# A batched 64x64 matmul: seven of sixteen input loads change their DMA queue

## The chip, the core and the metric

The kernel runs on one core of a Trainium2 chip. The metric is the device time of one execution in microseconds (us), lower is better. A core has five engines that work side by side, each through its own list of instructions in order: TensorE (PE in the profile, its weight loads PEld), VectorE (DVE), ScalarE (ACT), GpSimd (POOL) and SyncE (SP). Transfers between the device memory and the core's own memory are issued by one of SyncE, ScalarE and GpSimd, and are then carried out by the core's 16 DMA engines. The profile lists the transfers by the queue of the engine that issued them: q1 for SyncE, q10 for ScalarE, q0 for GpSimd.

## What is computed

```python
def reference(a, b):                       # both (1024, 64, 64), fp32
    return np.matmul(a, b).astype(np.float32)
```

That is 1024 independent products of 64 x 64 matrices. Each input and the output is 16.78 MB.

## The kernel before

The batch is cut into 16 tiles t of 64 matrices (1.05 MB of b and of the output each) and 8 slices s of 128 matrices of a (2.1 MB each), so that slice s serves tiles 2s and 2s+1. The products are taken in bf16 and summed in fp32.

**Loads.** `load_a(s)` (L69 to L78) brings three quarters of a slice by GpSimd's queue, with a cast to bf16 on the way (L73, three transfers that read 0.52 MB and write 0.26 MB each), and the fourth quarter as fp32 by SyncE's (L77). The first slice comes as fp32 by SyncE and ScalarE (L90). `load_b(t)` (L93) brings one tile of b as fp32 in one transfer (L96) into one of three buffers (`B_AHEAD = 3`): even tiles by SyncE's queue, odd ones by ScalarE's. Each of the 128 partitions gets 16 runs of 512 bytes.

**Work of a tile.** `regroup` (L108, L111; L105 for the first slice) puts a slice of a together in bf16 on VectorE; `transpose` (L120 on TensorE, L123 on ScalarE) transposes half of it; `spread(t)` (L133, four copies on VectorE) lays the transposed matrices out as block diagonals in `at_bd`; `cast(t)` turns the tile of b into bf16 (L144, on VectorE but for tile 0; the last tile in four pieces, L149 on VectorE and L151 on ScalarE). `multiply(t)` runs 64 matmuls (L189) in two halves and evacuates each half from PSUM with four copies (L177): on ScalarE, but for two of the eight copies of an odd tile, which VectorE makes; for the last tile four groups of four copies alternate between the two.

**Stores.** A tile's store is one transfer of 1.05 MB in runs of 1 KB (L166), on GpSimd's queue for tiles 0 to 13. Tile 14 goes out in two halves by SyncE, tile 15 in four quarters by ScalarE and SyncE in turn. It is issued one tile late (`HOLD = 2`). Output tiles have eight buffers.

**Order.** The order of the instructions is written out by hand, and each engine takes its own in that order; waits are put in where data or a free buffer is needed. One step t of the main loop reads:

```python
            if t + 1 < n_t:
                spread(t + 1)
                cast(t + 1)
            if t + B_AHEAD < n_t:
                load_b(t + B_AHEAD)
            if half == 0 and 0 < s < n_s - 1 - A_AHEAD:
                load_a(s + 1 + A_AHEAD)
```

then half a transposition, `multiply(t)`, `regroup` and transposition of a later slice, and `store(t - 1)`. Ahead of the loop stand the loads of tiles 0 to 2 of b and slices 0 to 2 of a; the loads of slices 3 and 4 follow the first multiplication. `load_b(t + 3)` fills the buffer of tile t, so it waits for `cast(t)`. On ScalarE an odd load stands, in order, between the evacuations of one tile and the work of the next. On GpSimd there are, besides the start's memsets, only transfers: the loads of a and the stores of tiles 0 to 13.

Of the kernel before, what the change touches and what calls it, by code (L numbers as in the profile page):

```python
# [13 lines left out]
def kernel(  # L14
# [14 lines left out]
    nc = tc.nc  # L29
# [62 lines left out]

    def load_b(t):  # L93
        b_sb = b_pool.tile([128, 16, 128], fp32, name="b_sb")
        queue = nc.scalar if t % 2 else nc.sync
        queue.dma_start(out=b_sb[:], in_=b_v[t])  # L96
        b_tiles[t] = b_sb

# [111 lines left out]
    with tc.manual_schedule():  # L210
        load_first_a()

        nc.vector.memset(warm[:, 0:1], 0.0)
        nc.scalar.copy(warm[:, 1:2], warm[:, 0:1])  # L214
        load_b(0)
        load_b(1)
        nc.vector.memset(bd_tiles[0][:], 0.0)  # L217
        make_identity(nc, identity)
        nc.gpsimd.memset(bd_tiles[1][:, 0], 0.0)
        load_a(1)  # L220
        load_b(2)
        nc.gpsimd.memset(bd_tiles[1][:, 1], 0.0)
        load_a(2)
# [63 lines left out]
```

## Time and profile before

| what | value |
|---|---|
| median of 3 runs | 135.0 us (134.95 to 135.19) |
| span of the profiled execution, first to last instruction | 133.1 us |
| median less span | 1.9 us |
| busy: VectorE, ScalarE, TensorE's matmuls, GpSimd | 94.5, 87.8, 65.7, 33.7 us |
| stores by GpSimd, 14 | median 22.3 us from issue to landing |
| loads of b by SyncE, 8, and by ScalarE, 8 | median 18.4 and 16.8 us from issue to landing |

The span is that of one execution taken by the hardware profiler; the execution's own time is its span and what lies around it, which the profile does not show, so the difference to the median stands for it. The page cuts the span into 40 equal slices; a digit is the busy share in tenths. "From issue to landing" holds the time a transfer stands in its queue as well as the moving. In a timeline, a line gives the start, the duration, the engine, the source line, the operation, what it writes and reads, and in brackets how long the engine stood idle before it and what ended that; a q after the engine's name marks its sequencer, which issues and waits.

### The profile page before, as it was taken

How to read it: one execution, taken by the hardware profiler on the slowest of the kernel's cores; microseconds unless marked ns; L12 is line 12 of the kernel's file. 1: busy time of each engine (PE TensorE's matmuls, PEld its weight loads, DVE VectorE, ACT ScalarE, POOL GpSimd, SP SyncE). 2: the span in 40 equal slices, each digit the busy share in tenths (PEclk: the TensorE clock that was granted, in tenths of full speed). 3: DMA queues.
4: the chain of work that ended last, by engine and by line, in shares of the span. 5: the costliest groups of instructions: out<-in, count | busy, mean ns of one | idle time of the engine just before them, and what ended most of it. 6: DMA issues, size and time to landing. Idle time of an engine off the chain costs nothing.

```text
span 133.1 us, 2837 instructions
## 1 busy us (share of the span) xinstructions
PE 65.7 (49%) x1152; PEld 62.7 (47%) x1152; DVE 94.5 (71%) x120; ACT 87.8 (66%) x161; POOL 33.7 (25%) x43
## 2 busy tenths in 40 slices
PE   0005504990068386059519672986199361776000
PEld 0005304980068275058509562975199360766000
DVE  5930299208999719598999699969999994978100
ACT  3134505899128999919899759696969987099600
POOL 8981000420082072143144022203020410210000
PEclk9999999999559999968996875579756985556855
DMA  3999999999999999999999999999999999999991
GB/s 75 367 332 311 307 312 279 278 307 326 328 307 402 316 322 334 393 385 401 318 282 365 402 397 356 308 307 387 395 396 387 393 396 391 402 403 402 380 339 41
DMA packets 19021, 45.01 MB, mean 338 GB/s; under 512 B 1088, under 2 KB 3136, under 8 KB 19008
## 3 DMA queue, kind: packets, MB, share of 16 engines
q0 software_dynamic: 6832, 20.19, 50.2%
q1 hardware_dynamic: 7120, 14.68, 30.5%
q10 hardware_dynamic: 5056, 9.96, 19.8%
q8 instruction: 9, 0.15, 0.4%
q14 instruction: 4, 0.03, 0.1%
HBM read 33.55 MB, written 16.78 MB: 378 GB/s over the span
## 4 chain that ended last, share of the span: by engine, by line
DMA 54%; DVE 18%; ACT 13%; issue 4%; PE 3%; SPq 1%; DVEq 0%; ACTq 0%
DMA b_sb<-in_b_dram 54%; ACT o_sb L177 9%; DVE at_bd L133 9%; DVE b_bf L144 4%; DVE o_sb L177 3%; PE at_ps L120 2%; ACT at_sb L123 2%; ACT b_bf L144 1%; PE o_ps L189 1%; DVE a_bf L108 1%; SPq L90 1%; DVE a_bf L111 1%; ACT b_bf L151 1%; SPq L96 0%; DVEq L133 0%
## 5 line engine op out<-in xcount | busy, mean ns | idle before, releaser
L177 ACT COPY o_sb<-o_ps 64x512 f32<-64x512 f32 x106 | 61.6, 581 | 9.5 <-PE o_ps L189 8.2
L189 PEld LDWEIGHTS <-at_bd 128*128 128x128 bf16 x1024 | 42.5, 113 | 39.7 <-DVE b_bf L144 26.8
L189 PE MATMUL o_ps<-b_bf,at_bd 128*128 128x64 bf16 x960 | 41.2, 213 | 36.0 <-DVE b_bf L144 25.1
L133 DVE COPY at_bd<-at_sb 32x1024 f32<-32x1024 f32 x64 | 46.6, 728 | 13.6 <-ACT at_sb L123 11.8
L120 PE MATMUL at_ps<-identity,a_bf 128*128 128x128 f32 x128 | 22.5, 350 | 19.3 <-ACT a_bf L105 11.4
L166 POOL DMA_DIRECT2D out_dram<-o_sb x14 | 16.3, 1166 | 55.4 <-ACT at_sb L123 23.0
L120 PEld LDWEIGHTS at_ps<-identity,a_bf 128*128 128x128 f32 x128 | 20.7, 190 | 19.4 <-issue 19.4
L144 DVE CAST b_bf<-b_sb 128x2048 bf16<-128x2048 f32 x14 | 17.5, 1249 | 10.0 <-DMA b_sb<-in_b_dram 9.8
L123 ACT COPY at_sb<-at_ps 128x512 f32<-128x512 f32 x32 | 17.4, 590 | 9.9 <-PE at_ps L120 7.6
L73 POOL DMA_DIRECT2D a_sb<-in_a_dram x21 | 13.3, 650 | 27.3 <-DVE a_bf L108 20.4
L177 DVE COPY o_sb<-o_ps 64x512 f32<-64x512 f32 x14 | 9.7, 690 | 0.3
L108 DVE COPY a_bf<-a_sb 128x3072 bf16<-128x3072 bf16 x7 | 7.4, 1059 | 0.0
L105 ACT CAST a_bf<-o_sb 128x1024 bf16<-128x1024 f32 x2 | 2.1, 1044 | 5.3 <-DMA o_sb<-in_a_dram 5.3
L111 DVE CAST a_bf<-a_raw 128x1024 bf16<-128x1024 f32 x7 | 4.8, 683 | 0.0
L144 ACT CAST b_bf<-b_sb 128x2048 bf16<-128x2048 f32 x1 | 1.9, 1897 | 4.1 <-DMA b_sb<-in_b_dram 4.1
L177 DVE COPY o_sb<-at_ps 64x256 f32<-64x256 f32 x8 | 3.4, 422 | 1.3 <-PE at_ps L189 1.2
L105 DVE CAST a_bf<-o_sb 128x1024 bf16<-128x1024 f32 x2 | 2.6, 1296 | 2.4 <-DMA o_sb<-in_a_dram 2.3
L189 PE MATMUL at_ps<-b_bf,at_bd 128*128 128x64 bf16 x64 | 3.6, 242 | 1.0 <-DVE at_bd L133 1.0
L217 DVE MEMSET at_bd<- 128x4096 f32 x1 | 3.5, 3472 | 0.8 <-issue 0.8
L151 ACT CAST b_bf<-b_sb 128x512 bf16<-128x512 f32 x2 | 1.1, 615 | 4.3 <-DMA b_sb<-in_b_dram 4.3
L177 ACT COPY o_sb<-at_ps 64x256 f32<-64x256 f32 x8 | 2.9, 367 | 0.1
L214 ACT ACT_TABLE_LOAD x1 | 1.3, 1283 | 2.3 <-issue 2.3
(12 smaller groups left out, 6.1 us busy)
## 6 DMA issues: line engine op xcount, KB each, us to landing
out_dram<-o_sb POOLq DMA_DIRECT2D x14, 1024.0 KB, 22.3
a_sb<-in_a_dram POOLq DMA_DIRECT2D x21, 256.0 KB, 16.4
a_raw<-in_a_dram SPq DMA_DIRECT2D x7, 512.0 KB, 19.1
o_sb<-in_a_dram SPq DMA_DIRECT2D x2, 512.0 KB, 6.2
o_sb<-in_a_dram ACTq DMA_DIRECT2D x2, 512.0 KB, 7.3
out_dram<-o_sb SPq DMA_DIRECT2D x2, 512.0 KB, 7.4
out_dram<-o_sb SPq DMA_DIRECT2D x2, 256.0 KB, 7.7
out_dram<-o_sb ACTq DMA_DIRECT2D x2, 256.0 KB, 5.9
```

The costliest lines, as they stand in the source:

```text
L73: nc.gpsimd.dma_start(out=a_sb[:, h, :, :].rearrange("p v k -> p (v k)"), in_=a_v[s, h])
L105: copy(a_bf[:, :, h, :], a_sb[h].rearrange("p (v k) -> p v k", v=16))
L108: nc.vector.tensor_copy(a_bf[:, :, 0:3, :], cast_sb[:].rearrange("p h v k -> p v h k"))
L111: nc.vector.tensor_copy(a_bf[:, :, 3, :], raw[:])
L120: nc.tensor.transpose(at_ps[:, vo, :], a_cols[:, 4 * vo + 2 * j + wl, :], identity[:])
L123: nc.scalar.copy(at_tiles[s][:, j, :, wl, :, :], at_ps[:].rearrange("p vo (g mp) -> p g mp vo", mp=4),)
L133: nc.vector.tensor_copy(bd[rows, :, :, :, h, :].rearrange("p j g wl mo -> p j (g wl) mo"), at_tiles[t // 2][rows, :, half, :, :, :].rearrange(
L144: (nc.vector.tensor_copy if t else nc.scalar.copy)(b_bf[:], b_sb[:])
L166: store_queue(t, lo).dma_start(out=o_v[t, :, lo : lo + n, :], in_=o_sb[:, lo : lo + n].rearrange("p gh j wl n -> p (gh j wl n)"),)
L177: copies[2 * par + wl](dst, src)
L189: nc.tensor.matmul(o_ps[:, gl, g % 2, j, :], at_bd[:, j, g, :, u], b_bf[:, g, 64 * u : 64 * u + 64], start=(u == 0), stop=(u == 1),)
L217: nc.vector.memset(bd_tiles[0][:], 0.0)
```

## The change

Odd tiles of b from tile 3 on are issued by GpSimd instead of ScalarE: seven transfers, 3, 5, 7, 9, 11, 13 and 15. Tile 1 stays on ScalarE's queue and even tiles on SyncE's. Shape, type and buffers are as before; the cast to bf16 stays where it was. In GpSimd's order the load stands where `load_b` stands in the loop: behind the store of tile t - 2 and ahead of the loads of a and the store of tile t - 1.

```diff
     def load_b(t):
         b_sb = b_pool.tile([128, 16, 128], fp32, name="b_sb")
-        queue = nc.scalar if t % 2 else nc.sync
+        queue = nc.sync if t % 2 == 0 else nc.scalar if t == 1 else nc.gpsimd
         queue.dma_start(out=b_sb[:], in_=b_v[t])
         b_tiles[t] = b_sb
```

## The prediction

> **What bounds the kernel now.** I read the page's slices first, then its queues.
>
> ```profile
> DMA  3999999999999999999999999999999999999991
> GB/s 75 367 332 311 307 312 279 278 307 326 328 307 402 316 322 334 393 385 401 318 282 365 402 397 356 308 307 387 395 396 387 393 396 391 402 403 402 380 339 41
> ...
> q0 software_dynamic: 6832, 20.19, 50.2%
> q1 hardware_dynamic: 7120, 14.68, 30.5%
> q10 hardware_dynamic: 5056, 9.96, 19.8%
> ...
> HBM read 33.55 MB, written 16.78 MB: 378 GB/s over the span
> ```
>
> The 16 DMA engines are busy 90% or more in every slice but the first and the last. The rate looks uneven because the loads of a that cast to bf16 are counted by the half they write: q0's 20.19 MB is 14.68 MB of stores plus 21 x 0.262 MB written by casting loads that read twice that. The three queues are GpSimd's (q0), SyncE's (q1) and ScalarE's (q10: 8 tiles of b and 1.57 MB besides). So the kernel is one transfer of 33.55 + 16.78 = 50.33 MB from first to last. Any change that moves the same bytes can only alter three things: the rate, holes in the stream, and its end.
>
> The windows (last two columns: DMA share, GB/s) give the rate without casting loads:
>
> ```profile
> 97.50:100.00 2.50, 2.50 (x42) 2.50 (x40) 2.41 (x4) 2.12 (x4) 0.31 (x1) 0.50 1.02 394
> 105.00:107.50 2.50, 0.00 (x0) 0.00 (x0) 2.44 (x4) 2.44 (x5) 0.04 (x1) 1.00 1.03 392
> 115.00:122.50 7.50, 6.02 (x110) 5.70 (x107) 6.07 (x13) 5.82 (x11) 1.35 (x1) 0.51 1.03 405
> 122.50:127.50 5.00, 0.00 (x0) 0.00 (x0) 1.26 (x3) 2.90 (x8) 0.00 (x0) 0.82 1.04 379
> 127.50:130.00 2.50, 0.00 (x0) 0.00 (x0) 0.00 (x0) 0.00 (x0) 0.00 (x0) 0.50 0.89 312
> ```
>
> Three queues together give 392, GpSimd's stores alone 405. From 127.5 us the stream thins (0.89 and 312): there the last store pieces, issued late, begin to set the time. Who issues them late is in ScalarE's timeline and the chain of waits:
>
> ```profile
> 116.54 1.14 ACT L151 CAST b_bf<-b_sb 128x512 bf16<-128x512 f32 x2 [4.28 <-DMA b_sb<-in_b_dram]
> 117.70 4.74 ACT L177 COPY o_sb<-o_ps 64x512 f32<-64x512 f32 x8
> 122.46 1.89 ACT L177 COPY o_sb<-at_ps 64x256 f32<-64x256 f32 x5
> ...
> 125.52 0.38 ACTq L166 DMA_DIRECT2D out_dram<-o_sb  x1
> ```
>
> ScalarE stands 4.28 us for tile 15 of b (the chain has it issued at 101.78 and landed at 116.46, 14.68 later). Then come 9.06 us of work to the last issue at 125.52. So stream and last chain end nearly together.
>
> **The change part by part.** The odd tiles from 3 to 15 are seven: 7 x 1.049 = 7.34 MB leave q10 for q0.
>
> *ScalarE loses* seven issues: MOVE_SHAPE of 0.02 us, its waits for VectorE's cast (2.0 us over two) and the gaps behind them ("issue", 2.1 us over three). I count 4.1 us of idle ScalarE gone, at nothing: ScalarE then waits longer for tile 15, which is late next.
>
> *GpSimd gains* seven issues. A store of 1024 runs of 1 KB takes it 0.90 us (at 109.24) to 1.85 (at 68.42); a load of a, 0.53. A tile of b is 2048 runs of 512 B, not in the trace: bounds 0.53 and 2 x 1.85 = 3.7 us, and I take 2 x 0.9 = 1.8, the plain store by its number of runs. 7 x 1.8 = 12.6 us stand beside 99 us in which GpSimd is idle. They cost nothing while older transfers wait in q0: its stores land a median 22.3 us after issue, more than six times even 3.7. If q0 ran dry, each would cost 1.8.
>
> The row shows GpSimd's store issue at 0.90 to 0.93 us alone and 1.35 to 1.37 beside VectorE's spreads. The Trainium skill's "SBUF — State Buffer", section "SBUF: two separate sides", speaks against the change here: a DMA issued from GpSimd stops being described while VectorE runs an fp32 SBUF copy, and one issued from ScalarE doesn't. By that rule each load could wait for one spread copy, 0.68 us by the page's fastest spreads, 7 x 0.68 = 4.8 us in all if bare. By the row it is 0.45 a store, under queued stores and so unseen.
>
> *VectorE* pays when GpSimd issues beside it: the regroup copy at L108 reads 0.95 alone and 1.32 in the two places where a store is issued beside it, so 0.37 a load, 2.6 us over seven. That is no path of its own (below).
>
> *GpSimd's order at the start.* The load of tile 3 stands before the loads of a's fourth slice and waits for the cast of tile 0, which ends at 21.6. These three issues now go at 8.3 to 11.6 and would go at about 24. Their slice is needed at 41.7 (L108). Behind the six earlier loads GpSimd's queue holds until 24, and q1 has work, so no hole. Tile 3 itself may come sooner than its 38.8. Cost: nothing; without that cover, 1 MB late is 2.7 us.
>
> *Queue depth.* GpSimd twice stands for an earlier transfer of its own to land (2.1 and 4.8 us, with eight in flight). It will do so more often, behind eight queued transfers: nothing.
>
> *SyncE* issues the same transfers in the same order. With q10 empty in the middle, q1 should hold a larger share, so even tiles, for which VectorE waits now (most of its 9.8 us in six waits, the longest 3.3), come sooner. In a full stream that is only an exchange of places: nothing.
>
> *The new order inside q0* is what costs. An odd tile now lands after every store issued before it. Landing times of single transfers, by their windows (last number: us from issue):
>
> ```profile
> b_sb<-in_b_dram ACTq DMA_DIRECT2D x1, 0.5 KB, 15.7
> out_dram<-o_sb POOLq DMA_DIRECT2D x1, 1024.0 KB, 28.0
> out_dram<-o_sb POOLq DMA_DIRECT2D x1, 1024.0 KB, 29.8
> out_dram<-o_sb POOLq DMA_DIRECT2D x1, 1024.0 KB, 21.2
> ```
>
> (each from a window of its own). The load is tile 11, issued at 77.29, so landed at 93.0. The stores are those of tiles 5, 6 and 10, issued at 68.42, 71.08 and 96.87: they land at 96.4, 100.9 and 118.1. In q0 tile 11 stands behind stores 5 and 6. At 93.0 some 1.9 MB of the two are not yet moved (store 6 whole, store 5 with 3.4 us to go beside other queues): 1.9/0.392 = 4.8 us, so near 97.8, while its cast starts now at 94.63. That is +3.2 for VectorE there. Of it 1.92 is taken back where VectorE waits for tile 14 (at 112.54), which then is no longer late. The rest, 1.3, reaches VectorE's last copies; these end at 123.8 against ScalarE's 125.5, so 1.7 are free: hidden. With the slower copies (tiles 13 and 15, 0.74) it is still about 2.0 against 1.7, so +0.3 at most.
>
> Tile 15 stands behind store 10, so it lands about when that store does, 118.1 instead of 116.46: +1.6 on ScalarE's last chain, and the last issue goes to 127.1. What that does to the end lies between two rows. The last pieces now take 5.7 us (ScalarE's) to 7.5 us (SyncE's) to land in a full stream; with the same wait, +1.6. But a quiet landing is shorter: the first load, 0.52 MB beside another 0.52, lands in 4.5 us, of which 1.05/0.392 = 2.7 is the moving, so 1.8 fixed; 0.26 MB alone would be an estimated 1.8 + 0.7 = 2.5, so 129.6, before today's last landing near 131.8: +0. The nearest row is the window from 127.5: 0.89 busy, so nearer to full than to quiet, and about a third of a delay shows. I take +0.5.
>
> *Rate.* From 392 to 405 for 7.34 MB gains 18.72 - 18.12 = 0.6; from 392 to 379, the slowest full window, loses 0.64. Two queues (97.5, 394) read like three (392), so I take 0.
>
> Sum: 133.1 + 0.5 + 0 = 133.6 for the span. The median is 135.0, so 1.9 lie outside the span, unchanged: **135.5**.
>
> **Rivals.**
>
> 1. *No change (135.0).* Stores to be moved are plenty behind tile 15 (11 to 15, 5.24 MB = 13.4 us), the late issue is wholly covered. For it: landing of 5.7 to 7.5 where 2.5 would do. Against: the thinning after 127.5.
>
> 2. *Faster (134.3).* The mechanism is packets: GpSimd's stores run at 405 alone, the mixture at 392. If a tile of b runs in q0 like a store, 0.6 are gained for 7.34 MB; if all that is moved between 25 and 115 us (90 x 0.392 = 35.3 MB) goes at the two-queue 394, another 90.0 - 89.6 = 0.4. Together 1.0 at most; taken at 0.7. It decides where windows from 60 to 115 us without casting loads read 397 or more and tile 15 lands no later than 117. Against: two queues read 394 only.
>
> 3. *Clearly slower (137).* Odd tiles fall so far behind in q0 that VectorE, which waits for nothing else late in the kernel, becomes the bound: +4.8 at tile 11 instead of +3.2, and 2.6 for slower copies, less 1.9 and 1.7 taken back: +3.8 at the most, 138.8; about half of it, +2, is this rival's time. It decides when VectorE's idle time before L144, 9.8 us now, doubles, and slices before the last two fall under 9.
>
> 4. *It doesn't do what it says*: ScalarE is relieved, but ScalarE waits for data at the end, so relief alone gives 0. That is contained in the first two.
>
> The skill's "DMA: Bandwidth & Descriptors", section "Issuing engines are not separate DMA queues", has all queues run on the same 16 engines, so that another issuer saves issue time alone: by it the sum would be 135.0. The trace shows that the place in a queue matters as well, since store 10, issued 4.9 us before tile 15, lands 1.6 us after it.
>
> **How the numbers follow.** Forecast (slightly slower, 135.3 to 136.3) 0.37; no change 0.20; faster (133.8 to 134.7) 0.28; clearly slower (136.3 to 138.8) 0.15. About 0.2%, 0.27 us, is what a measurement can tell from no change. So faster 0.28, same 0.20, slower 0.52. The range reaches from 134.2 (most of rival 2's 1.0) to 137.2 (135.0 with the tail's full 1.6 and the rate's 0.64), which leaves out some 0.08 on each side. The forecast's own range is 135.3 to 136.3.
>
> **What would show it.** Right: q0 near 27.5 MB, q10 near 2.6; DMA digits still 9; tile 11 landing at 96 to 100, tile 15 near 118; ScalarE's wait before L151 longer or its cast after 118; last issue near 127. Wrong: tile 15 landing at or before 116.5, a hole in the DMA row, GpSimd's issue of a tile of b over 3.7 us, or a rate over 400 in the middle.

## The result, and the profile after

The changed kernel takes 141.34 us (141.25 to 141.52) against 134.97 of the kernel before, +6.4 us; the ratio over all runs is 1.0488, 95% interval 1.0461 to 1.0515. The prediction was 135.5, range 134.2 to 137.2. Times here and below are medians, and differences in us are differences of medians; the ratios are taken over the runs and can lie some 0.2% beside them.

The profile's span grew from 133.1 to 139.2, by 6.1, so the loss is inside it. The slices and queues of the page after:

```profile
DMA  3999999999999999999999999999999999999991
GB/s 87 380 323 308 306 312 301 347 342 297 271 253 312 391 300 286 280 395 389 317 304 272 404 370 289 232 380 384 321 365 395 337 379 400 359 381 397 364 361 37
...
q0 software_dynamic: 8736, 27.53, 64.7%
q1 hardware_dynamic: 7120, 14.68, 30.5%
q10 hardware_dynamic: 1360, 2.62, 5.0%
...
HBM read 33.55 MB, written 16.78 MB: 362 GB/s over the span
```

The bytes are those announced (27.53 and 2.62 MB), and the DMA digits are the same as before, all 9: no hole. Yet the rate over the span fell from 378 to 362. The engines are as busy as before and move less. Late slices, where no casting load is left to blur the count, read 321, 337 or 359 beside others of 395 to 400. The windows there (last two columns: DMA share, GB/s) show where:

```profile
97.50:102.50 5.00, 1.09 (x32) 1.00 (x32) 2.92 (x4) 4.77 (x9) 1.36 (x1) 0.94 1.03 323
102.50:107.50 5.00, 2.15 (x41) 2.15 (x42) 3.40 (x5) 0.22 (x1) 0.89 (x1) 0.50 1.03 397
107.50:112.50 5.00, 4.39 (x80) 4.06 (x78) 4.76 (x7) 4.90 (x10) 1.12 (x1) 0.88 1.03 343
112.50:117.50 5.00, 1.75 (x47) 1.63 (x47) 4.84 (x7) 4.91 (x9) 1.43 (x2) 0.81 1.03 393
120.00:122.50 2.50, 1.52 (x30) 1.36 (x28) 1.47 (x2) 2.17 (x4) 0.00 (x0) 0.50 1.02 336
122.50:127.50 5.00, 3.24 (x59) 2.96 (x57) 4.83 (x8) 3.26 (x6) 1.36 (x1) 0.50 1.01 394
```

Windows near 395 and windows near 335 alternate. The landings of two of the moved loads (last number: us from issue) say what the latter are:

```profile
b_sb<-in_b_dram POOLq DMA_DIRECT2D x1, 1024.0 KB, 22.8
b_sb<-in_b_dram POOLq DMA_DIRECT2D x1, 1024.0 KB, 12.7
```

They are tile 11, issued at 81.15 and landed at 104.0, and tile 15, issued at 111.38 and landed at 124.1; tile 13 between them, issued at 96.27, landed at 113.5. The windows with the low rate are those just before a moved tile lands: GpSimd's queue is then at that tile. Against 397 the first of them loses 5 x (1 - 323/397) = 0.93 us, the third window 0.68, the fifth 0.38: 2.0 us in the middles of three such stretches, out of seven. ScalarE's timeline at the end is that of before, moved by 7.6 us (116.54 to 124.18, and 125.52 to 133.15):

```profile
124.18 1.14 ACT L151 CAST b_bf<-b_sb 128x512 bf16<-128x512 f32 x2 [1.96 <-DMA b_sb<-in_b_dram]
...
133.15 0.38 ACTq L166 DMA_DIRECT2D out_dram<-o_sb  x1
```

### The profile page after: what moved, and what is told of

It reads as the page before. It is cut to its first block, busy times and chain, and to the rows that moved or that the text cites. A ratio compares the mean times of both kernels' runs of the same rounds, so it can differ in the third digit from the quotient of the medians.

```text
span 139.2 us, 2826 instructions
## 1 busy us (share of the span) xinstructions
PE 66.0 (47%) x1152; PEld 63.0 (45%) x1152; DVE 95.2 (68%) x120; ACT 87.3 (63%) x154; POOL 43.1 (31%) x50
## 3 DMA queue, kind: packets, MB, share of 16 engines
q0 software_dynamic: 8736, 27.53, 64.7%
q10 hardware_dynamic: 1360, 2.62, 5.0%
## 4 chain that ended last, share of the span: by engine, by line
DMA 69%; ACT 7%; DVE 6%; issue 5%; POOL 3%; PE 3%; SPq 1%; DVEq 0%; POOLq 0%; ACTq 0%
DMA b_sb<-in_b_dram 46%; DMA a_sb<-in_a_dram 14%; DMA out_dram<-o_sb 8%; ACT o_sb L177 6%; PE o_ps L189 3%; DVE at_bd L133 2%; DVE b_bf L144 2%; POOL a_sb L73 2%; ACT b_bf L144 1%; POOL b_sb L96 1%; DVE o_sb L177 1%; SPq L90 1%; DVE a_bf L108 1%; ACT b_bf L151 0%; DVE a_bf L111 0%
## 5 line engine op out<-in xcount | busy, mean ns | idle before, releaser
L189 PEld LDWEIGHTS <-at_bd 128*128 128x128 bf16 x1024 | 44.8, 116 | 47.8 <-DVE b_bf L144 32.6
L189 PE MATMUL o_ps<-b_bf,at_bd 128*128 128x64 bf16 x960 | 43.4, 218 | 43.8 <-DVE b_bf L144 31.0
L120 PE MATMUL at_ps<-identity,a_bf 128*128 128x128 f32 x128 | 20.7, 330 | 19.5 <-ACT a_bf L105 11.0
L120 PEld LDWEIGHTS at_ps<-identity,a_bf 128*128 128x128 f32 x128 | 18.7, 175 | 19.5 <-issue 19.5
L144 DVE CAST b_bf<-b_sb 128x2048 bf16<-128x2048 f32 x14 | 17.2, 1227 | 13.6 <-DMA b_sb<-in_b_dram 13.3
L166 POOL DMA_DIRECT2D out_dram<-o_sb x14 | 15.5, 1108 | 27.6 <-ACT o_sb L177 14.8
L96 POOL DMA_DIRECT2D b_sb<-in_b_dram x7 | 9.2, 1310 | 37.1 <-DVE b_bf L144 17.7
L73 POOL DMA_DIRECT2D a_sb<-in_a_dram x21 | 14.3, 694 | 17.2 <-DMA b_sb<-in_b_dram 9.6
L111 DVE CAST a_bf<-a_raw 128x1024 bf16<-128x1024 f32 x7 | 5.4, 773 | 0.0
L144 ACT CAST b_bf<-b_sb 128x2048 bf16<-128x2048 f32 x1 | 1.9, 1898 | 4.1 <-DMA b_sb<-in_b_dram 4.1
```

The source lines that it names most:

```text
L73: nc.gpsimd.dma_start(out=a_sb[:, h, :, :].rearrange("p v k -> p (v k)"), in_=a_v[s, h])
L111: nc.vector.tensor_copy(a_bf[:, :, 3, :], raw[:])
L120: nc.tensor.transpose(at_ps[:, vo, :], a_cols[:, 4 * vo + 2 * j + wl, :], identity[:])
L144: (nc.vector.tensor_copy if t else nc.scalar.copy)(b_bf[:], b_sb[:])
L166: store_queue(t, lo).dma_start(out=o_v[t, :, lo : lo + n, :], in_=o_sb[:, lo : lo + n].rearrange("p gh j wl n -> p (gh j wl n)"),)
L189: nc.tensor.matmul(o_ps[:, gl, g % 2, j, :], at_bd[:, j, g, :, u], b_bf[:, g, 64 * u : 64 * u + 64], start=(u == 0), stop=(u == 1),)
```

## The experiments

The first theory was **A**: runs of 512 bytes move more slowly when GpSimd's queue describes them. Its rivals were **B**, that two queues do less than three, and **C**, that the odd tiles' place behind GpSimd's stores is what costs.

**Odd tiles by SyncE** (r1_sp):

```diff
-        queue = nc.sync if t % 2 == 0 else nc.scalar if t == 1 else nc.gpsimd
+        queue = nc.scalar if t == 1 else nc.sync
```

> Odd tiles of b from 3 on go by SyncE's queue, so GpSimd's queue holds what it held before and two queues work in the middle, as in the changed kernel. Theory A (512-byte runs described by GpSimd move more slowly): no loss from GpSimd, the stream stays at 390 to 400 GB/s, time 134 to 136.5 us. Rival B (two queues instead of three, or ScalarE's queue missing): slow like the change, 140 to 142. Rival C (the place of the odd tiles behind GpSimd's stores and loads of a): they stand behind even tiles of b and quarters of a instead, so at most 1 to 2 us over before, 135 to 137.

Measured: 139.39 us, ratio 1.0313 (1.0277 to 1.0348). All three missed. GpSimd carries no tile of b here, and two thirds of the loss (4.4 us) are still there. Its windows show both kinds again, late in the kernel:

```profile
90.00:92.50 2.50, 0.29 (x10) 0.30 (x11) 2.44 (x4) 2.25 (x4) 0.00 (x0) 1.00 1.05 318
102.50:105.00 2.50, 0.41 (x8) 0.42 (x9) 1.74 (x3) 1.66 (x3) 0.52 (x1) 0.54 1.06 302
```

In the first of these the list of queues has q1 alone (0.79 MB) and nothing from q0: SyncE's tiles of b, with no store beside them, go at 318 with the engines full. So A as it was put falls, and **D** was formed: 512-byte runs are slow on any queue where nothing but such runs is in flight, and are carried at nearly full rate where longer work goes beside them.

Not all of this run's loss is rate, though. Its slices have holes near the end, which the change hasn't:

```profile
DMA  3999999999999999999999999999999999997985
```

From 122.5 to 132.5 us the engines are busy 0.89, 0.83, 0.99 and 0.73 in steps of 2.5 us, so 1.4 us stand idle; the kernel before has 0.3 us of that kind (the 0.89 from 127.5). So about 1.1 of the 4.4 us is holes and not the rate; that they come of the tiles' place in SyncE's queue, rival C's kind, is likely and not shown.

**The same change with long rows** (r2_pool_8k, and r3_pool_1k with g=8, u=4 in place of g=1, u=32; r4_act_8k is r2 with `nc.scalar` for the moved tiles):

```diff
+        moved = t % 2 and t >= 3
+        queue = nc.sync if t % 2 == 0 else nc.gpsimd if moved else nc.scalar
+        b_w = b.rearrange("(t g y) (kp u) n -> t (y kp) g (u n)", g=1, y=64, u=32)
+        if moved:
+            queue.dma_start(
+                out=b_sb[:].rearrange("p (g x) c -> p g (x c)", g=1), in_=b_w[t]
+            )
...
```

What changes besides the length of a run: a partition's 512-byte runs lie 64 KB apart in b, r3's 1 KB runs 128 KB apart, and a row of 8 KB is one piece; and GpSimd's issue of a moved tile is shorter (0.54 to 0.86 us in r2, 1.15 or more in the change).

> As the changed kernel, but each partition of a moved tile gets one row of 8 KB instead of 16 runs of 512 bytes; so the moved tiles are read in another order and their products are others. Bytes, queue, order and waits are the same. Theory A (short runs): the loss of 6.4 us goes, 134 to 136; the windows that fell to 296 to 340 GB/s read 390 or more. Rivals B and C (number of queues; order in GpSimd's queue and its waits): unchanged, 140 to 142.

Measured: 135.29 us, ratio 1.0020 (1.0000 to 1.0039). Queue, bytes, waits and order are those of the change, and nearly all of the loss is gone (6.1 of 6.4 us). Where the changed kernel read 323 and 343, this one reads about 400, with its own moved tiles (11, then 13) in flight:

```profile
92.50:97.50 5.00, 1.53 (x47) 1.32 (x43) 3.69 (x5) 4.92 (x10) 1.50 (x2) 0.85 1.02 399
102.50:107.50 5.00, 3.89 (x76) 3.56 (x74) 4.83 (x7) 4.92 (x10) 0.57 (x1) 0.97 1.01 401
```

> As the changed kernel, but a moved tile is read in 8 runs of 1 KB to a partition instead of 16 of 512 bytes, in another order, so the products of these tiles are others. Theory A with a cost for each run: half of the runs, half of the loss or less, 135 to 138; if the cost is a threshold between 512 bytes and the 1 KB of the stores, none of it, 134 to 136. Rivals B and C: unchanged, 140 to 142.

Measured: 138.06 us, ratio 1.0219 (1.0192 to 1.0247). The loss is about half (2.2% of 4.9%), just over the upper end of what a cost by run would give. The pages of r3 and of the change both list 8736 packets on q0, so the number of packets isn't what makes the difference.

> The control for the rows of 8 KB: as the kernel before (odd tiles on ScalarE's queue), but the odd tiles from 3 on are read as one row of 8 KB to a partition, in another order, so the products of these tiles are others. Theory A: run length matters on GpSimd's queue alone, so 134 to 135.3. If run length matters on any queue, this is faster than before by 1 us or more, and the loss of the change isn't GpSimd's own.

Measured: 133.69 us, ratio 0.9912 (0.9878 to 0.9946). Long rows gain on ScalarE's queue too, 1.3 us, but far less than the 6.1 between the change and r2. So run length (with the addresses that go with it) matters on either queue, and nearly five times as much where GpSimd's queue carries the tiles.

**The rates by themselves** (m1_rates). The body of the kernel is left out; what stands in its place is (comments added here)

```python
        short(nc.sync, s1, 0)          # four tiles of b, 16 runs of 512 bytes
        barrier()
        short(nc.gpsimd, s1, 4)
        barrier()
        long(nc.sync, s1, 8)           # four tiles, one row of 8 KB
...
        short(nc.gpsimd, s1, 4)
        copies(14)                     # fp32 copies of 128 x 1024 on VectorE
```

> No product is computed: stages of 4 tiles to a queue, each stage begun when the one before has landed. b in 512-byte runs by SyncE alone; by GpSimd alone; b in 8 KB rows by SyncE; by GpSimd; four stores by GpSimd; short runs by SyncE and ScalarE at once; by SyncE and GpSimd at once; short runs by SyncE beside GpSimd's stores; short runs by GpSimd beside fp32 copies on VectorE; at last short runs by SyncE and ScalarE beside eight stores by GpSimd. Theory A: short runs by GpSimd 300 GB/s or less, by SyncE and by SyncE with ScalarE 380 or more. Theory D: short runs 290 to 340 on any queue and any pair, 8 KB rows and stores about 400, short runs beside stores 385 or more. Rival E (VectorE's copies hold up GpSimd's describing): GpSimd's stage is fast alone and slower by a fifth beside the copies.

Windows inside the stages (last two columns as before; the first columns are VectorE's, ScalarE's and GpSimd's busy time), in the order of the expectation; this kernel was run once:

```profile
17.50:25.00 7.50, 0.00 (x0) 0.00 (x0) 0.00 (x0) 1.00 1.06 290
35.00:42.50 7.50, 0.00 (x0) 0.00 (x0) 0.00 (x0) 1.00 1.03 292
50.00:57.50 7.50, 0.00 (x0) 0.00 (x0) 0.00 (x0) 1.00 1.00 424
65.00:70.00 5.00, 0.00 (x0) 0.00 (x0) 0.00 (x0) 1.00 1.03 433
77.50:85.00 7.50, 0.00 (x0) 0.00 (x0) 0.00 (x0) 1.00 1.01 336
95.00:115.00 20.00, 0.00 (x0) 0.40 (x1) 0.00 (x0) 1.00 1.06 290
127.50:145.00 17.50, 0.00 (x0) 0.00 (x0) 0.00 (x0) 1.00 1.04 290
160.00:170.00 10.00, 0.00 (x0) 0.00 (x0) 0.00 (x0) 1.00 1.03 397
185.00:192.50 7.50, 5.70 (x9) 0.00 (x0) 0.00 (x0) 1.00 1.02 290
205.00:235.00 30.00, 0.00 (x0) 0.34 (x1) 0.00 (x0) 1.00 1.03 393
```

Short runs go at 290 to 292 on SyncE's queue, on GpSimd's, and on either pair, with or without VectorE: D in every stage but that of the stores alone (336 instead of 400), and neither GpSimd nor the copies are the cause. The window from 185 lies behind GpSimd's issues, which ran beside the copies from 179.02:

```profile
28.41 4.72 POOL L42 DMA_DIRECT2D s<-in_b_dram  x4 [27.97 <-DVE o L62]
179.02 4.91 POOL L42 DMA_DIRECT2D s<-in_b_dram  x4 [22.97 <-DVE s L60]
```

Four issues took 4.91 us beside copies and 4.72 without, and the stage as a whole, from the first issue to the first instruction that waited for its end, 17.8 us (to 196.77) against 17.9 (28.41 to 46.28). So rival E falls as well. Rows of 8 KB go at 424 and 433. Beside GpSimd's stores the same short runs bring the sum to 397, and three queues to 393, which is the rate the kernel before holds. The share of busy time is 1.00 to 1.06 in all of them: it can't tell 290 from 433.

**Long rows for the even tiles instead** (r5_even_8k): the moved tiles keep their short runs, SyncE's get rows of 8 KB.

```diff
+        if t % 2 == 0 and t >= 2:
+            queue.dma_start(out=b_sb[:].rearrange("p g c -> p (g c)"), in_=b_w[t])
```

> The changed kernel, with the odd tiles on GpSimd's queue in runs of 512 bytes as there; but the even tiles from 2 on, on SyncE's queue, are read as one row of 8 KB to a partition, in another order, so the products of those tiles are others. Theory A (GpSimd's short runs are slow by themselves, whatever goes beside them): the loss stays but for what even tiles gain anywhere, 139 to 141. Theory D (short runs are slow where nothing but short runs is in flight, on whichever queue; GpSimd's queue holding a tile of b means that the stores no longer fill the gaps): the two queues never hold short runs at once, so most of the loss goes, 133.5 to 137.

Measured: 137.18 us, ratio 1.0156 (1.0127 to 1.0186): two thirds of the loss gone, which A did not allow, but just above D's range. SyncE's faster tiles are soon done, and then GpSimd's short runs are alone: from 97.5 to 100 us, just before a moved tile lands at 100.6, only q0 moves bytes and the rate is 364. From 107.5 to 110, with the next moved tile on its way (it lands at 111.4) and SyncE's rows of 8 KB beside it, it is 393: longer work that is a load helps as a store does.

**ScalarE takes stores in exchange** (r6_store_act):

```diff
         if t < n_t - 2:
-            return nc.gpsimd
+            return nc.scalar if t % 2 else nc.gpsimd
```

> The changed kernel with an exchange: GpSimd takes the odd tiles of b from 3 on as there, and ScalarE issues the stores of the odd tiles 1 to 13 in their place. So three queues carry traffic in the middle, and a store can be in flight while both other queues hold tiles of b. Theory A: GpSimd's short runs stay slow, 139 to 143. Theory D: part of the loss comes back, 135 to 138.5; not all, since ScalarE's stores run dry at times and ScalarE stands behind its own work to issue them.

Measured: 139.40 us, ratio 1.0311 (1.0277 to 1.0344): a third comes back, less than D's range, and the number lies inside A's. From 97.5 to 100 us, with tiles of b in both other queues, ScalarE's stores moved 0.12 MB of 0.87 and the rate was 347. That they are too small a part of the mixture to fill it is the likely reason; it wasn't shown.

**Three tiles moved** (r7_three: 5, 9 and 13).

```diff
-        queue = nc.sync if t % 2 == 0 else nc.scalar if t == 1 else nc.gpsimd
+        queue = nc.sync if t % 2 == 0 else nc.gpsimd if t in (5, 9, 13) else nc.scalar
```

> Only tiles 5, 9 and 13 go by GpSimd's queue; 3, 7, 11 and 15 stay on ScalarE's. Both theories: a loss for each moved tile, so 3/7 of 6.4 us, 137.2 to 138.2. Theory D somewhat less, since ScalarE's queue holds a tile at times. A loss of the order (the last tile behind a store) would be gone altogether here, as tile 15 isn't moved: 134.5 to 135.5.

Measured: 137.85 us, ratio 1.0214 (1.0183 to 1.0245), 0.97 us a tile against 0.91 with seven. The loss goes about by the tile, and tile 15, which wasn't moved, is no special part of it. Some 0.5 us of it are a hole near the end, though (busy 0.92 and 0.75 in two steps from 125 to 130 us), so by rate alone it is nearer to 0.8 a tile. The window from 82.5 to 85, with tiles of b on GpSimd's and ScalarE's queues and hardly anything from SyncE (0.04 of 0.80 MB), reads 319: the pair with SyncE is nothing special either.

**All tiles from 2 on by GpSimd** (r10_all_pool), against a last rival, F, that two queues with short runs get in each other's way:

```diff
-        queue = nc.sync if t % 2 == 0 else nc.scalar if t == 1 else nc.gpsimd
+        queue = nc.sync if t == 0 else nc.scalar if t == 1 else nc.gpsimd
```

> All tiles of b from 2 on go by GpSimd's queue, as runs of 512 bytes; SyncE keeps the quarters of a and the last stores. Theory D (512-byte runs move at 290 GB/s wherever nothing else is in flight): up to 14 tiles at 1.049/0.290 - 1.049/0.397 = 0.97 us each, less where a quarter of a goes beside them, so 142 to 149. Rival F (the pair of GpSimd's and SyncE's queues, both with short runs, is what is slow): the pair is never at it together, so 135 to 138.

Measured: 142.94 us, ratio 1.0595 (1.0576 to 1.0614). F falls: one queue alone loses as well. Its windows from 95 to 120 us average

```profile
95.00:120.00 25.00, 14.28 (x272) 13.55 (x272) 22.13 (x27) 18.14 (x33) 8.47 (x7) 0.80 1.02 362
```

with q0 alone in flight (9.04 of 9.06 MB), tiles and stores in turn. The loss is 0.57 us for each of 14 tiles, at the low end of what D gave.

**What is left with long rows.** r2 is 1.2% (1.6 us) slower than its control r4, with the same rows on ScalarE's queue. Two runs put one tile each of r2 back on ScalarE's, tile 3 or tile 15.

```diff
-        queue = nc.sync if t % 2 == 0 else nc.gpsimd if moved else nc.scalar
+        queue = nc.sync if t % 2 == 0 else nc.gpsimd if t >= 5 else nc.scalar        # r8
+        queue = nc.sync if t % 2 == 0 else nc.gpsimd if 3 <= t < 15 else nc.scalar   # r9
```

> Where the 0.3 us over before, and 1.6 over the control on ScalarE's queue, go that are left with rows of 8 KB. Odd tiles from 3 on are read as one row of 8 KB to a partition (in another order, so their products are others); tile 3 goes by ScalarE, 5 to 15 by GpSimd. If the start costs it (GpSimd stands for the cast of tile 0 with the loads of a's fourth slice behind it, and SyncE's short runs are alone for about 5 us at 355 to 365 GB/s, 0.5 us by the windows): 134.6 to 134.9. If only the late tiles matter: 135.2 to 135.4.

Measured: 134.43 us, ratio 0.9967 (0.9949 to 0.9985), 0.9 us under r2 (0.5%, 0.7 us, by the ratios) and a little under the range named for the start: the start does cost.

> As the run before it in this list, but tile 15 goes by ScalarE and 3 to 13 by GpSimd. If the place of the last tile behind the store of tile 10 is what costs (the term of 0.5 us of the prediction): 134.0 to 134.8. If the start or the middle costs it: 135.2 to 135.4.

Measured: 135.84 us, ratio 1.0072 (1.0056 to 1.0089), 0.5% *over* r2 and over both ranges. Giving the last tile its old place doesn't help, but the run isn't a clean test of that place: with the tile gone, GpSimd's queue runs dry and there is a hole that r2 hasn't:

```profile
120.00:122.50 2.50, 1.34 (x26) 1.18 (x24) 2.38 (x5) 2.44 (x5) 1.23 (x1) 0.50 0.62 231
```

No run points to a version that computes the products and beats the kernel before; r4 and r8 are faster only because they read b in an order that its products can't use.

## Why the prediction was wrong

1. *"The kernel is one transfer ... can only alter the rate, holes in the stream, and its end."* Right, and it was the rate.

2. *The rate term is the step that failed.* It was taken at 0, because "two queues (97.5, 394) read like three (392)", with bounds of -0.6 and +0.64 from windows at 405 and 379. The window at 97.5 held ScalarE's tile of b beside GpSimd's stores, as the list of its queues has it:

```profile
q0 software_dynamic: 166, 0.64, 66.2%
q10 hardware_dynamic: 165, 0.34, 35.1%
q1 hardware_dynamic: 6, 0.01, 0.9%
```

In the kernel before, GpSimd's queue never carried b, so a store or a load of a went beside the short runs. The change puts b in that queue too, and none of the rows that the prediction read showed short runs alone. The runs put 290 there (m1) and 302 to 343 in the windows shown of the kernels. The bound from the nearest rows was not a bound. Seven tiles at 290 instead of 397 would be an estimated 7 x (1.049/0.290 - 1.049/0.397) = 6.8 us; the change measures 6.4. That these are so near is partly luck, since the windows read more than 290 and SyncE's bytes beside the tiles are slowed with them. With rows of 8 KB 6.1 of the 6.4 go (r2); 1.3 of these are gained on ScalarE's queue as well (r4), so 4.8 are what the short runs cost for being in GpSimd's queue, and the other 1.6 are the queue and the place. Whether it is the length of a run or the distance between the runs in b that makes them slow, no run separates.

3. *The place in the queue.* Tile 11 was put at 97.8 and tile 15 at about 118. In the change they land at 104.0 and 124.1, but in r2, with the same order and rows of 8 KB, at 98.5 and 116.9 (its landing rows, issued at 78.18 and 105.97, are the next two lines):

```profile
b_sb<-in_b_dram POOLq DMA_DIRECT2D x1, 1024.0 KB, 20.3
b_sb<-in_b_dram POOLq DMA_DIRECT2D x1, 1024.0 KB, 10.9
```

So where the rate is what the prediction took it for, the reckoning by what stands ahead in the queue held within 1.3 us; for tile 15 that is partly luck, since it was issued at 105.97 and not at the 101.78 of the kernel before. The price put on it, +0.5 at the tail, is not shown either way: with long rows the change of queue costs 1.6 us in all (r2 against r4), and r9, which gives tile 15 its old place back, takes longer, but with a hole of its own. Tile 3's part is in the next point; what makes up the rest is open.

4. *GpSimd's start, "cost: nothing".* The cover named was that SyncE's queue has work. It had, but short runs alone; r8 gets 0.7 to 0.9 us back by leaving tile 3 where it was. That the slow rate under this cover makes it up is argued from the rates, not shown by itself.

5. *GpSimd's issues*, taken at 1.8 us each and unseen: 1.31 on average, and m1 shows no cost of theirs in time (292 by GpSimd, 290 by SyncE). *VectorE beside them*: the rule in the Trainium skill's "SBUF — State Buffer", section "SBUF: two separate sides", would have let the copies hold up GpSimd's describing; in m1 the stage beside copies took 17.8 us against 17.9 without, so no run here shows it in the time. *Rival 3*: VectorE's idle time before L144 went from 9.8 to 13.3 us, not to the double, and no slice fell under 9: it waits because the stream is slow, and is not the bound. *Queue depth*, also taken at nothing: GpSimd stood for earlier transfers of its own for 22 us instead of 6.9, but in r2, where nearly all of the loss is gone, still for 18; whether it has a part in r2's 1.6 us is open.

6. *ScalarE's relief at nothing*: nothing came of it that any run shows. *VectorE's slower copies*, put at 2.6 us and hidden: its busy time rose by 0.7 only, from 94.5 to 95.2 us.

A rule of the Trainium skill would have led the same wrong way: "DMA: Bandwidth & Descriptors", section "Specifications", gives 512 bytes as enough for line rate. Here 512-byte runs alone move at 290 and 8 KB rows at 424 to 433, so the measurement decides.

## What to carry to other kernels

A queue that always carries long work may be what keeps short runs on the other queues at full rate: before moving a load into it, ask what will be in flight beside the load at each moment, and find a row of the trace in which such runs were alone before pricing it at the mixture's rate. Read the rate next to the share of busy DMA time, since the share stays at 9 or over 1.00 whether the engines move 290 or 433 GB/s. Where reading in longer runs is possible, one run with a rearranged order shows what the short runs cost, with the queue and its order kept; the addresses change along with the length.

## What was not expected of the hardware

- 512-byte reads in 128 partitions move at the same 290 GB/s from one queue or two, whoever issues them; 1 KB runs give back about half of the loss (r3), and with stores beside them the sum is 397. Why the mixture hides it, the profile doesn't show.
- Four of GpSimd's stores alone moved at 336 GB/s in m1, where the stores alone near the end of the kernel before read 405. This was not followed up.
